# One decoder layer on one core: scores in larger groups, keys loaded ahead, probabilities in whole rows, padded products

## The chip, the cores and the metric

The kernel runs on one core of one Trainium2 chip. The metric is the device time of one execution in microseconds; the time before is the median of three runs.

## The reference

The kernel computes one layer of a hybrid decoder. There are two groups of tokens: a prompt of 512 tokens, and 8 running sequences with one new token each (the sample). All of it is float32. Cut to what matters:

```
def mixer_layer(x, s0, k_past, v_past, w_in, w_alpha2, b_alpha, gla_norm_g, w_out, ln_g, ln_b, rel_bias):
    h = jnp.einsum('btd,de->bte', x, w_in)
    qa, ka, va, za, ga, qb, kb, vb, gb = jnp.split(h, split_points, axis=-1)
    log_a = jax.nn.log_sigmoid((jnp.einsum('btr,rk->btk', za, w_alpha2) + b_alpha).astype(F32)) / GATE_TEMP
    o_a, s_new = gla_chunked(qa, ka, va, log_a, s0, chunk)
    o_a = o_a * lax.rsqrt(jnp.mean(jnp.square(o_a), axis=-1, keepdims=True) + RMS_EPS) * gla_norm_g.astype(F32)
    ...
        o_b = prompt_dilated(qb, kb, vb, rel_bias)
    ...
        o_b = dilated_attention(qb, k_all, v_all, q_idx, rel_bias)
    mix = jnp.concatenate([o_a * jax.nn.silu(ga.astype(F32)), o_b * jax.nn.silu(gb.astype(F32))], axis=-1)
    y = jnp.einsum('bte,ed->btd', mix.astype(x.dtype), w_out)
    x_new = layer_norm(DEEPNORM_ALPHA * x + y, ln_g, ln_b)
```

`gla_chunked` is gated linear attention with 4 heads; `dilated_attention` has 8 heads, each of which sees three patterns of past keys with a bias by distance. For the sample the keys and values of 1024 past tokens come from a cache; 256 of them fall into a pattern.

## The kernel before

**Planner.** The program's order is made on the host by `Plan`. Each piece of work is a generator (`Task`) with a priority; it yields operations, requests for a buffer (`Need`, or `Pair` for several at once) or waits for a mark (`At`). `Plan.run` goes through the tasks in order of priority, lets each take its buffers (`advance`), and issues the operation that by its own costs (`Op`) can start first. Every engine then executes its instructions in this fixed order. Line 359 in `Plan.issue` is where every instruction is issued, so nearly all rows of the profile have L359, and one goes by the names of the tiles. Nearly all DMAs are issued on SP, one queue, in order.

**Buffers.** `SLOTS` and `BANKS` are the supply: two raw weight buffers (`r`), six for their split halves (`w`), four 4 KB buffers for the sample (`sv`), three strips (`st`), four probability tiles (`pr`), and the eight PSUM banks as `d` 3, `s` 3, `t` 2.

**Products.** A float32 operand is split into a rounded high part (ACT, `hi`) and a low remainder (DVE, `lo`), and a product is three matmuls: high by high, high by low, low by high (`three`). `dense` is the backbone on PE: projections in the order ka, za, qa, qb, kb, vb, gb, va, ga over 8 tiles of the model dimension, then the output projection (`ps_yf`, `ps_y`). `first_loads` and `first_splits` bring x and the ka weights at the start. Everything else is put between the projections: GLA by levels (`ps_l`), state and output (`gla_state`, `gla_out`, `ps_oa`), and the attention of the prompt.

**Attention of the prompt.** `strips` loads a skewed bias strip per head; `scores` makes the scores (`ps_s`) of one feature tile, that is two heads, for query tiles 0 and 1 (`pi` 0) or 2 and 3 (`pi` 1), `softmax` follows with the bias, exponentials and transposes (`ps_pt`), `weighted` with the values (`ps_pv`).

**Attention of the sample.** `sample_queries` transposes the queries, writes them to DRAM (`qsd`), and per sequence loads them back to all partitions (`qbc`) with the past keys (`past`, 512 KB). GpSimd multiplies, DVE adds up (`lt`). `sample_softmax` makes the probabilities and writes them to DRAM (`psd_s`). `sample_values` loads per sequence the past values (`vv`) and the probabilities to all partitions (`pb`), GpSimd multiplies, DVE adds up (`o_pv`). The result enters the mix before the output projection. The loads of `pb` before, two per sequence for 64 partitions each:

```
            row = psd_s[bi * 8:bi * 8 + 8, :]
            for h2 in range(2):
                yield D.dma_start(pb[h2 * 64:h2 * 64 + 64],
                                  bass.AP(tensor=row.tensor, offset=row.offset + h2 * 256, ap=[[0, 64], [512, 4], [1, 256]]))
```

An access pattern is a list of pairs, step and count, the outermost first.

Of the kernel before, what the change touches and what calls it, by code (L numbers as in the profile page):

```python
# [48 lines left out]
C_W = 419  # L49
# [5 lines left out]

N_WARM = 8
# [133 lines left out]
class Plan:  # L190
# [173 lines left out]
def trunk(ctx: ExitStack, tc: tile.TileContext, xT, xp, xs, state, ck, cv, w_in, wab, gnorm,  # L364
# [23 lines left out]
    def rsqrt(o, x, scale, eps, between=None):  # L388
# [3 lines left out]
        yield V.tensor_scalar(x, x, scale, eps, op0=ALU.mult, op1=ALU.add)  # L392
        yield S.activation(o, x, AF.Ln)
        yield S.activation(o, o, AF.Exp, scale=-0.5)
        if between:

            add(between, 5)
            yield S.activation(t, o, AF.Square)
            yield S.mul(t, t, x)
            yield S.activation(t, t, AF.Copy, scale=-0.5, bias=1.5)  # L400
            yield S.mul(o, o, t)
        else:
            yield V.tensor_tensor(t, o, o, op=ALU.mult)
# [22 lines left out]
    rb = cst("rb", [66, NB, HB], F32R)  # L426
# [5 lines left out]
    q_s, k_s = cst("q_s", [P, 4, NB]), cst("k_s", [P, 4, NB])  # L432
    q_rows = cst("q_rows", [32, P])
    vnt, vat = cst("vnt", [P, 4, NB]), cst("vat", [P, 4, NB])
    lt = cst("lt", [P, 2, 64])
# [6 lines left out]
    psd_s = dram.tile([64, 256], F32, name="psd_s")  # L442
# [63 lines left out]
    def weight_loads():  # L506
        for g in order:
            for i in range(g.parts):
                yield from g.load(i)
# [26 lines left out]
    def first_loads():  # L536
        za = w_in[:, OFF["za"]:OFF["za"] + 16].rearrange("(k p) n -> p k n", p=P)
        for n, a, *b in FIRST:
# [10 lines left out]
            mark("first")  # L549
        yield D.dma_start(zw[:, :, :16], za)  # L550
# [3 lines left out]
        B["rb_raw"] = yield Need("t1", "rb_raw", [64, NB, HB])  # L554
        for i in range(2):
            yield D.dma_start(B["rb_raw"][i * 32:i * 32 + 32], rel_bias[:, None, :].to_broadcast([32, NB, HB]))
# [6 lines left out]
    def first_splits():  # L563
        for j, (n, a, *b) in enumerate(FIRST):
            yield At("first", j + 1)
            if n == "x":
# [6 lines left out]
                yield from split(xraw[a // 2][:, a % 2, c], xh[a][:, c], xl[a][:, c])  # L573
                mark("xs")
# [106 lines left out]
    def dense():  # L681
# [101 lines left out]
    def bias_table():  # L783
# [9 lines left out]
        yield At("rb")  # L793
        pt = yield bank("t", "ps_tab")
# [103 lines left out]
    def gla_state():  # L898
# [23 lines left out]
        plan.share(st, 3)  # L922
# [19 lines left out]
    def gla_queries():  # L942
# [12 lines left out]
        for h2 in range(2):  # L955
            plan.share(B[f"att{h2}"], 2)
        for u in range(2):
            yield from make(f"oa{u}", Need("g", f"oa{u}", [P, 2, 512]), 2)
            add(gla_out(u), 26 + u)

    def gla_out(u):

        yield At("st", 2 * u + 1)
        yield At("dg")
        va, att, qd = B[f"va{u}"], [B[f"att{h2}"] for h2 in range(2)], B["qa"]
        ps = yield Pair(*(bank("s", f"ps_oa{u}{h2}") for h2 in range(2)))
        po = {(h2, j, m): ps[h2][:, (2 * j + m) * P:(2 * j + m) * P + P] for h2 in range(2) for j in range(2) for m in range(2)}
        mm = Batch(T.matmul(po[h2, j, m], att[h2][:, (2 * u + j) * 2 + m, :], va[:, j, (m * 2 + h2) * P:(m * 2 + h2) * P + P],
                            start=j + m == 0, stop=False, skip_group_check=True) for h2 in range(2) for j in range(2) for m in range(2))
        mm += [T.matmul(po[h2, j, m], qd[h2 * 64:h2 * 64 + 64, m, (2 * u + j) * P:(2 * u + j) * P + P],  # L970
                        B["st"][h2 * 64:h2 * 64 + 64, 2 * u + j - 1, m, :], start=False, stop=j + m == 2, skip_group_check=True)
               for j in range(2) for m in range(2) for h2 in range(2) if u + j]
        yield mm
        free(qd, B["st"], *att)
        plan.share(va, 2)
        for h2 in range(2):
            plan.share(ps[h2], 2)
        for j in range(2):
            add(gla_head(u, j, ps, po), 26 + u + j / 2)
# [116 lines left out]
    def strips():  # L1096
        yield At("tab")
        yield At("qb", 1)
        for pi in range(2):
            w = 256 * (pi + 1)  # L1100
            for h in range(HB):
                yield At(f"kb{h // 2}{pi}")
                strip = yield Need("st", f"strip{h}{pi}", [P, w])
                plan.share(strip, 2)
# [6 lines left out]
    def scores(m, pi, qt):  # L1111
# [9 lines left out]
        for v in range(2):  # L1121
            yield At(f"strip{2 * m + v}{pi}")
        yield At(f"qb{m}{pi}")
        for u in range(pi + 1):
            yield At(f"kb{m}{u}")
        every = [(v, q) for v in range(2) for q in (qt if own else qt[:1])]
        pr = yield Pair(*(Need("pr", f"pr{2 * m + v}{q}", [P, (q + 1) * P if own else n]) for v, q in every))
        ps = yield Pair(*(bank(("s", "d"), f"ps_s{2 * m + v}{q}") for v, q in every))
        pr, ps = ({(v, q): z[every.index((v, q if own else qt[0]))] for v in range(2) for q in qt} for z in (pr, ps))
        kp, qx = B[f"kp{m}"], [B[f"q{x}{pi}"] for x in "hl"]  # L1130
        yield Batch(T.matmul(ps[v, q][:, cols[q]], qx[a][v * 64:v * 64 + 64, m, (q % 2) * P:(q % 2) * P + P],
                             kp[v * 64:v * 64 + 64, b, :(q + 1) * P], start=i == 0, stop=i == 2, skip_group_check=True)
                    for q in qt for i, (a, b) in enumerate(((0, 0), (0, 1), (1, 0))) for v in range(2))
        free(kp, *qx)
        for v in range(2):
            if not own:
                plan.share(ps[v, qt[0]], len(qt))
                plan.share(pr[v, qt[0]], len(qt))
            for q in qt:
                add(softmax(2 * m + v, q, ps[v, q], pr[v, q], cols[q]), 31 + 20 * pi / 100 + m / 50)  # L1140
# [70 lines left out]
    def sample_queries():  # L1211
        yield At("qb", 8)
        yield from sample_rows(q_s, q_rows)
        yield D.dma_start(by_tile(qsd), q_rows)
        for bi in range(NB):
            qbc = yield Need("t2", f"qbc{bi}", [P, 512])
            yield D.dma_start(qbc, qsd[bi:bi + 1, :].to_broadcast([P, 512]))
            past = yield Need("sv", f"past{bi}", [P, 2, 512])
            yield D.dma_start(past, ck[bi])
            add(sample_logit(bi, past, qbc), 50)  # L1220

    def sample_logit(bi, past, qbc):
# [4 lines left out]
        yield V.tensor_reduce(lt[:, :, bi * 8:bi * 8 + 8], past.rearrange("p k (h d) -> p k h d", d=64), axis=AX.X, op=ALU.add)  # L1227
# [3 lines left out]
    def sample_softmax():  # L1231
        yield At("kb", 8)
        yield At("lt", 5)
        sel = yield Need("t1", "sel", [64, C_AV - C_E2])
        yield D.dma_start(sel, c_f[:64, C_E2:C_AV])
        e2, pnm, m32 = sel[:, :P], sel[:, C_PN - C_E2:C_PN - C_E2 + 32], sel[:32, C_LN - C_E2:]
# [7 lines left out]
        l32 = yield Need("t1", "l32", [32, NB * HB])  # L1244
        yield V.tensor_reduce(ln_new, prod.rearrange("p (h d) -> p h d", d=64), axis=AX.X, op=ALU.add)
        free(prod)
        yield V.tensor_tensor(l32.rearrange("p (r u) -> p r u", u=2), ln_new[:, None, :].to_broadcast([32, 32, 2]),
# [9 lines left out]
        yield T.matmul(ps[:64, :258], rb.rearrange("p b h -> p (b h)"), cts, start=True, stop=False, skip_group_check=True)  # L1257
        yield T.matmul(ps[:64, 256:257], l32, one[:32], start=False, stop=False, skip_group_check=True)
# [456 lines left out]
```

## Time and profile before

| | |
|---|---|
| median of three runs | 289.32 us (288.43 to 290.51) |
| profiled execution | 288.67 us |
| its span | 286.8 us |
| PE busy | 275.0 us, 96% |
| DVE, ACT, GpSimd busy | 225.7, 167.5, 55.9 us |
| granted TensorE clock | 0.994 |
| DMA | 51.18 MB, mean 178 GB/s |
| first matmul to last | 1.20 us to 279.26 us |

The profile is of one execution. The span goes from its first to its last instruction; the device time is longer by what lies around it. PE is TensorE, PEld its weight loads, DVE, ACT, POOL and SP the vector, scalar, GpSimd and sync engines. A window row gives for a stretch its length, the busy time of each engine with the count of instructions, the granted clock, the mean share of 16 DMA engines and what they moved. Float32 products without a split appear as two matmuls each.

### The profile page before, as it was taken

The page shows a single profiled execution, that of the slowest core. Times are in us where ns is not written, and L with a number is a line of the kernel's source. Part 1 is how long each engine was busy: PE and PEld are TensorE (multiplying, and loading weights), DVE is VectorE, ACT ScalarE, POOL GpSimd, SP SyncE. Part 2 cuts the span into 40 slices and gives each one's busy share as a digit, 9 for nine tenths or more (in the row PEclk, how much of TensorE's full clock was granted, in tenths as well). Part 3 has the DMA queues.
Part 4 walks back from the last instruction along what each step waited for, and adds up shares of the span by engine and source line. Part 5 has one row for each costly group of instructions (what it writes and reads, how often), then busy time and mean ns, then how long its engine had stood idle before and what let it go on. Part 6 is the DMA issues. An engine that isn't in the chain of part 4 may idle for free.

```text
span 286.8 us, 6896 instructions
## 1 busy us (share of the span) xinstructions
PE 275.0 (96%) x2636; PEld 259.5 (90%) x2636; DVE 225.7 (79%) x547; ACT 167.5 (58%) x478; POOL 55.9 (19%) x74
## 2 busy tenths in 40 slices
PE   8999999999999998999999999999999999999990
PEld 5899999998989998899989999999999999997880
DVE  3846897999889968988889997864888995339745
ACT  5757664554567777566869867526689774113201
POOL 4000001000782444401604444540000000000000
PEclk9999999999999999999999999999999999999997
DMA  7966522225866797648998987559754788741211
GB/s 209 269 191 195 147 75 75 75 78 167 296 201 222 196 287 230 175 130 243 274 201 188 239 227 219 149 149 228 221 95 148 230 297 252 111 151 73 78 75 73
DMA packets 58936, 51.18 MB, mean 178 GB/s; under 512 B 12555, under 2 KB 50197, under 8 KB 58903
## 3 DMA queue, kind: packets, MB, share of 16 engines
q1 hardware_dynamic: 58794, 50.66, 63.2%
q8 instruction: 21, 0.34, 0.5%
q14 instruction: 13, 0.10, 0.1%
q10 hardware_dynamic: 108, 0.07, 0.1%
HBM read 45.17 MB, written 6.03 MB: 179 GB/s over the span
## 4 chain that ended last, share of the span: by engine, by line
PE 71%; DVE 13%; DMA 8%; ACT 5%; issue 2%; SPq 1%; DVEq 0%; ACTq 0%
PE ps_qb L359 8%; PE ps_yf L359 8%; PE ps_y L359 8%; PE ps_ga L359 6%; PE ps_kb L359 4%; PE ps_qa L359 4%; PE ps_gb L359 4%; PE ps_va L359 4%; PE ps_ka L359 4%; DMA raw_gb__2152<-in_w_in_dram 3%; DMA out_dram<-feat 3%; PE ps_pt L359 2%; PE ps_va_f L359 2%; PE ps_l L359 2%; PE ps_s L359 2%; PE ps_pv L359 2%
## 5 line engine op out<-in xcount | busy, mean ns | idle before, releaser
L359 POOL TENSOR_TENSOR vv<-vv,pb 128x256 f32<-128x256 f32 x32 | 26.1, 846 | 45.5 <-DMA pb<-psd_s 39.8
L359 POOL TENSOR_TENSOR past<-past,qbc 128x256 f32<-128x256 f32 x32 | 25.6, 831 | 43.4 <-DMA past<-in_ck_dram 36.0
L359 ACT ACTIVATE pr<-pr,ms 128x128 f32<-128x128 f32 (+3 forms) x49 | 26.1, 546 | 5.8 <-DVE ms L359 5.2
L359 PE MATMUL ps_pt<-cf,pr 128*128 128x128 f32 x80 | 14.1, 280 | 1.4 <-DVE pt L359 1.0
L359 DVE CUSTOM_DVE_ANT_0 pr<-ps_s,strip 128x128 f32<-128x128 f32 (+3 forms) x32 | 14.3, 476 | 0.0
L359 PE MATMUL ps_ka<-xx,hi_ka 128*128 128x264 f32 (+1 forms) x64 | 13.5, 307 | 0.3 <-DVE xx L359 0.3
L359 ACT ACTIVATE sg<-sg 128x264 f32<-128x264 f32 (+1 forms) x32 | 13.4, 419 | 0.2
L359 PEld LDWEIGHTS ps_ka<-xx,hi_ka 128*128 128x128 f32 x64 | 11.0, 205 | 1.2 <-DVE xx L359 0.8
L359 DVE TENSOR_TENSOR ptl<-ps_pt,pth 128x384 fp32r<-128x384 f32 (+1 forms) x16 | 9.8, 617 | 2.8 <-ACT pth L359 2.8
L359 PEld LDWEIGHTS ps_pt<-cf,pr 128*128 128x128 f32 x80 | 9.0, 140 | 3.3 <-DVE pt L359 1.6
L359 ACT ACTIVATE d<-d 128x512 f32<-128x512 f32 x13 | 7.8, 637 | 6.7 <-DVE d L359 6.7
L359 ACT COPY feat_y<-ps_yf 128x256 f32<-128x256 f32 x8 | 3.0, 371 | 12.7 <-PE ps_yf L359 12.7
L359 ACT ACTIVATE rstd<-mv 128x1 f32<-128x1 f32 x4 | 0.7, 199 | 15.9 <-DVE mv L359 15.9
L359 POOL MEMSET att<- 64x512 f32 x2 | 1.0, 523 | 44.5 <-DVE ks L359 44.5
L359 ACT CAST pth<-ps_pt 128x384 fp32r<-128x384 f32 (+1 forms) x16 | 8.4, 534 | 2.2 <-PE ps_pt L359 2.0
L359 DVE TENSOR_REDUCE o_pv<-vv 128x4 f32<-128x1024 f32 x8 | 9.7, 1212 | 0.0
L359 DVE TENSOR_REDUCE lt<-past 128x16 f32<-128x1024 f32 x8 | 9.6, 1199 | 0.0
L359 PE MATMUL ps_ka<-xx,lo_ka 128*128 128x264 f32 (+1 forms) x32 | 9.4, 295 | 0.0
L359 DVE TENSOR_TENSOR obT<-ps_pv,pvl 64x256 f32<-64x256 f32 x16 | 6.6, 415 | 3.5 <-ACT pvl L359 3.3
L359 DVE TENSOR_TENSOR xx<-x_raw,xx 128x520 fp32r<-128x520 f32 (+2 forms) x9 | 5.8, 640 | 4.6 <-ACT xx L359 4.6
L359 ACT COPY pvl<-ps_pv 64x256 f32<-64x256 f32 x16 | 5.5, 370 | 6.1 <-PE ps_pv L359 5.3
L359 DVE TENSOR_TENSOR d<-b 128x1024 f32<-128x1024 f32 x7 | 8.5, 1218 | 0.0
(535 smaller groups left out, 1092.4 us busy)
## 6 DMA issues: line engine op xcount, KB each, us to landing
past<-in_ck_dram SPq DMA_DIRECT2D x8, 512.0 KB
vv<-in_cv_dram SPq DMA_DIRECT2D x8, 512.0 KB
pb<-psd_s SPq DMA_DIRECT2D x16, 256.0 KB
qbc<-qsd SPq DMA_DIRECT2D x8, 256.0 KB
strip<-tabr SPq DMA_DIRECT2D x8, 256.0 KB
y<-in_xp_dram SPq DMA_DIRECT2D x4, 512.0 KB
x_raw<-in_xT_dram SPq DMA_DIRECT2D x7, 260.0 KB
out_dram<-y SPq DMA_DIRECT2D x3, 512.0 KB
```

The lines of the kernel that those rows point to most:

```text
L359: getattr(eng.eng, op.fn)(*op.args, **op.kw)
```

## The change

- `Plan.run`: when a task's step frees a buffer, the pass through the tasks starts again from the first in line.
- `first_splits`, `dense`: x tiles 1 and 2 are split in two halves as tile 0 was (`N_HALF`), and the ka products that need the low part of x come last in each step. The first weight group after ka is loaded ahead of `zw`.
- `scores`, `strips`: for `pi` 0 two feature tiles, four heads, in one batch, with four banks and four `pr` at once; two heads' strips share a buffer.
- `gla_out`: both halves in one batch with four banks.
- `sample_queries`: the first four `past` are loaded once the first qb tile is there, ahead of the queries' way through DRAM.
- `sample_softmax`, `sample_values`: `psd_s` is laid out by sequence and half, written in two DMAs, and each `pb` is one load for 128 partitions in rows of 4 KB.
- The small products `ps_sl`, `ps_pn`, `ps_ms`, `ps_vs` are padded to 128 by 128, with tiles cleared or widened for it (`rb`, `lt`, `sel`, `l32`, `pn_r`, `sums`, `avg`).
- `rsqrt` for the last normalisation has one ACT instruction less; the bias table's product waits for the first qa result; `a_s` takes the place of `la_s`.

```
-            for t in sorted(self.tasks, key=lambda t: (t.prio, t.seq)):
-                if not self.advance(t):
+            line = sorted(self.tasks, key=lambda t: (t.prio, t.seq))
+            self.freed = True
+            while self.freed:
+
+                self.freed = False
+                for t in line:
+                    self.advance(t)
+                    if self.freed:
+                        break
...
+            yield V.tensor_scalar(x, x, eps, -0.5, op0=ALU.add, op1=ALU.mult)
+            yield S.activation(o, x, AF.Ln, scale=-2.0)
+            yield S.activation(o, o, AF.Exp, scale=-0.5)
             add(between, 5)
             yield S.activation(t, o, AF.Square)
-            yield S.mul(t, t, x)
-            yield S.activation(t, t, AF.Copy, scale=-0.5, bias=1.5)
+            yield S.activation(t, t, AF.Copy, scale=x, bias=1.5)
             yield S.mul(o, o, t)
...
+        yield from order[0].load(0)
         yield D.dma_start(zw[:, :, :16], za)
...
-                yield from split(xraw[a // 2][:, a % 2, c], xh[a][:, c], xl[a][:, c])
-                mark("xs")
+                for c in (c,) if b or a >= N_HALF else TS:
+                    yield from split(xraw[a // 2][:, a % 2, c], xh[a][:, c], xl[a][:, c])
+                    mark("xs")
...
-                yield At("xs", k + 1 + (u if k == 0 else 1))
-                for i in range(2):
-                    yield from three(pk[i, u][:, :TW[u]], k, halves(k, u, groups[f"ka{i}"]))
+                yield At("xs", 2 * k + 1 + u if k < N_HALF else k + 1 + N_HALF)
+
+                for last in (False, True):
+                    for i in range(2):
+                        pairs = halves(k, u, groups[f"ka{i}"])
+                        for j in (1,) if last else (0, 2):
+                            yield T.matmul(pk[i, u][:, :TW[u]], *pairs[j], start=k == 0 and j == 0, stop=k == KT - 1 and last)
...
     def sample_queries():
-        yield At("qb", 8)
-        yield from sample_rows(q_s, q_rows)
-        yield D.dma_start(by_tile(qsd), q_rows)
+        yield At("qb", 2)
+        pasts = []
         for bi in range(NB):
-            qbc = yield Need("t2", f"qbc{bi}", [P, 512])
-            yield D.dma_start(qbc, qsd[bi:bi + 1, :].to_broadcast([P, 512]))
+            if bi == 4:
+                yield At("qb", 8)
+                yield from sample_rows(q_s, q_rows)
+                yield D.dma_start(by_tile(qsd), q_rows)
+                for i, past in enumerate(pasts):
+                    yield from sample_query(i, past)
             past = yield Need("sv", f"past{bi}", [P, 2, 512])
             yield D.dma_start(past, ck[bi])
-            add(sample_logit(bi, past, qbc), 50)
+            if bi < 4:
+                pasts.append(past)
+            else:
+                yield from sample_query(bi, past)
...
-        yield T.matmul(ps[:64, :258], rb.rearrange("p b h -> p (b h)"), cts, start=True, stop=False, skip_group_check=True)
-        yield T.matmul(ps[:64, 256:257], l32, one[:32], start=False, stop=False, skip_group_check=True)
+        yield T.matmul(ps[:, :258], rb.rearrange("p b h -> p (b h)"), cts, start=True, stop=False, skip_group_check=True)
+        yield T.matmul(ps[:, 256:257], l32, one, start=False, stop=False, skip_group_check=True)
...
-        yield D.dma_start(psd_s, p_s[:, :256])
+
+        for h2 in range(2):
+            src = bass.AP(tensor=p_s.tensor, offset=p_s.offset + h2 * p_s.ap[0][0], ap=[[2 * p_s.ap[0][0], 32], [1, 256]])
+            yield D.dma_start(psd_s[:, h2].rearrange("b (m k) -> b m k", m=4), src)
...
-            row = psd_s[bi * 8:bi * 8 + 8, :]
-            for h2 in range(2):
-                yield D.dma_start(pb[h2 * 64:h2 * 64 + 64],
-                                  bass.AP(tensor=row.tensor, offset=row.offset + h2 * 256, ap=[[0, 64], [512, 4], [1, 256]]))
+            row = psd_s[bi]
+            yield D.dma_start(pb, bass.AP(tensor=row.tensor, offset=row.offset, ap=[[1024, 2], [0, 64], [1, 1024]]))
...
-            if h % 2 == 0:
-                for qt in ((2, 3) if pi else (0, 1),):
-                    add(scores(h // 2, pi, qt), 31 + 20 * pi / 100 + h / 100)
+            if h % (2 if pi else 4) == 0:
+                add(scores((h // 2,) if pi else (h // 2, h // 2 + 1), pi, (2, 3) if pi else (0, 1)), 31 + 20 * pi / 100 + h / 100)
```

More of the change, by code (lines that the diff above doesn't have):

```diff
@@ L441, in trunk @@
     qsd = dram.tile([NB, 512], F32, name="qsd")
[L442 removed]
+    psd_s = dram.tile([NB, 2, 1024], F32, name="psd_s")
     B = {}
@@ L506, in weight_loads @@
     def weight_loads():
-        for g in order:
+        for g in order[1:]:
             for i in range(g.parts):
@@ L1120, in scores @@
         own = pi
[L1121 to L1135, printed above, removed]
+        heads = [2 * m + v for m in ms for v in range(2)]
@@ new lines, in scores @@
+        for h in heads:
+            yield At(f"strip{h}{pi}")
+        for m in ms:
+            yield At(f"qb{m}{pi}")
+            for u in range(pi + 1):
+                yield At(f"kb{m}{u}")
+        every = [(h, q) for h in heads for q in (qt if own else qt[:1])]
+        pr = yield Pair(*(Need("pr", f"pr{h}{q}", [P, (q + 1) * P if own else n]) for h, q in every))
+        ps = yield Pair(*(bank(("s", "d"), f"ps_s{h}{q}") for h, q in every))
+        pr, ps = ({(h, q): z[every.index((h, q if own else qt[0]))] for h in heads for q in qt} for z in (pr, ps))
```

136 lines of the change are left out of this document (82 added, 54 removed).

## The prediction

> **What bounds the kernel now.** I read the page first, then the waits of PE, then windows of stages, and last the chain that ended last.
>
> ```profile
> span 286.8 us, 6896 instructions
> PE 275.0 (96%) x2636; PEld 259.5 (90%) x2636; DVE 225.7 (79%) x547; ACT 167.5 (58%) x478; POOL 55.9 (19%) x74
> PE 71%; DVE 13%; DMA 8%; ACT 5%; issue 2%; SPq 1%; DVEq 0%; ACTq 0%
> ```
>
> PE is busy 96% of the span, and 71% of the chain is PE. An edit gains only if it takes time out of PE's stream or closes one of its few gaps; it loses as soon as PE's next operand comes late. The profiled execution took 288.67 us, 1.87 us more than its span and 0.65 us under the median of the three runs, 289.32 us; the sum below is made against 288.67.
>
> The gaps are small. Where operands came late, it was behind a DMA:
>
> ```profile
> 2.60 3.77 DMA x_raw<-in_xT_dram
> ...
> 102.77 8.52 DMA out_dram<-feat
> 111.28 0.02 issue
> 111.31 0.37 ACT pvl L359
> 111.68 0.52 ACT hi_vb__1819 L359
> ...
> 113.58 0.88 DVE lo_vb__1820 L359
> ...
> 132.90 9.72 DMA raw_gb__2152<-in_w_in_dram
> ```
>
> Columns: start, duration, what. A transfer with little ahead of it takes 3.77 us; the weight load at 132.90 took 9.72 us, because it was issued behind four probability loads:
>
> ```profile
> 129.56 1.32 SPq L359 DMA_DIRECT2D pb<-psd_s  x2
> 130.97 0.55 SPq L359 DMA_DIRECT2D vv<-in_cv_dram  x1
> 131.62 1.23 SPq L359 DMA_DIRECT2D pb<-psd_s  x2
> 132.90 0.60 SPq L359 DMA_DIRECT2D raw_gb__2152<-in_w_in_dram  x1
> ```
>
> So nearly all loads go through SP's one queue, and a weight load waits for what stands ahead of it. This decides the forecast. The windows that I need (length, busy times, clock, DMA share, GB/s):
>
> ```profile
> 27.00:28.00 1.00, 1.00 (x10) 1.00 (x9) 0.97 (x4) 0.76 (x2) 0.00 (x0) 1.00 0.52 205
> 252.40:254.00 1.60, 1.60 (x15) 1.60 (x15) 0.17 (x1) 0.37 (x1) 0.00 (x0) 1.00 1.01 399
> 126.40:182.00 55.60, 55.12 (x459) 52.50 (x458) 49.94 (x118) 40.70 (x105) 19.14 (x25) 1.00 0.88 220
> 100.00:110.00 10.00, 10.00 (x89) 9.99 (x88) 7.51 (x22) 7.29 (x24) 2.94 (x4) 1.00 0.98 282
> 110.00:120.00 10.00, 8.65 (x67) 7.39 (x66) 9.21 (x20) 5.46 (x16) 6.92 (x8) 1.00 0.70 212
> 40.00:60.00 20.00, 20.00 (x386) 19.59 (x386) 17.64 (x27) 9.70 (x19) 1.05 (x2) 1.00 0.29 78
> 110.00:240.00 130.00, 127.87 (x1104) 122.23 (x1103) 110.42 (x285) 91.24 (x267) 33.00 (x40) 1.00 0.75 202
> ```
>
> **The parts that should gain.** First, the start. The halved splits of x tiles 1 and 2, with the product that needs the low part put last:
>
> ```profile
> 6.39 0.62 ACT L359 CAST xx<-x_raw 128x520 fp32r<-128x520 f32 x1 [0.76 <-DMA x_raw<-in_xT_dram]
> 7.05 0.70 DVE L359 TENSOR_TENSOR xx<-x_raw,xx 128x520 fp32r<-128x520 f32 x1 [0.96 <-ACT xx L359]
> 7.07 0.39 PE L359 MATMUL ps_ka<-xx,hi_ka 128*128 128x264 f32 x1
> 7.80 0.39 PE L359 MATMUL ps_ka<-xx,hi_ka 128*128 128x264 f32 x1 [0.34 <-DVE xx L359]
> ```
>
> PE issues one product of tile 1 at 7.07 and stands until DVE has the low part, 7.80. With halves, ACT has the first at about 6.8, four products need only high parts of x (4 x 0.12 = 0.48 us), and DVE's first half is there by 7.3: 0.7 us. Tile 2 gives 0.2 more. I take 0.9 (0 to 1.2). The price, two more instructions each on ACT and DVE, lies under PE's first 10 us. The weight load put ahead of `zw` delays that by 512 KB, 1.3 us at 399 GB/s; its products start 9.7 us after its issue:
>
> ```profile
> 8.56 0.38 SPq L359 DMA_DIRECT2D zw<-in_w_in_dram  x1
> ...
> 18.30 1.98 PE ps_za L359 x62
> ```
>
> Second, visits to another matmul shape (rows by columns of the array):
>
> ```profile
> 82.80 5.28 PE ps_kb L359 x44
> 88.08 0.89 PE ps_s L359 x12
> ...
> 123.64 0.90 PE ps_sl L359 x7
> ...
> 200.98 2.43 PE ps_oa L359 x24
> ```
>
> A full product of about 256 columns costs 5.28/44 = 0.12 us. The twelve score products run as six pairs, three of 256 and three of 128 columns, 0.54 us of work in 0.89: a visit costs up to 0.35 us, entry and exit together. The change saves seven: two by joining feature tiles in `scores`, one by joining the halves in `gla_out`, four by padding (`ps_sl`, `ps_pn`, `ps_ms`, `ps_vs`). At 0.2 to 0.35 each that is 1.4 to 2.5; I take 1.6, since `ps_sl` has only 0.90 us in all.
>
> Third, the keys ahead: four loads of 512 KB move into 40 to 60 us, where DMA is busy 0.29, out of the traffic that fills it to 0.98 in 100 to 110. Its victim is the store that landed after 8.52 us, held ACT's `pvl` and cost PE 1.35 us in 110 to 120. I take 1.0 (0 to 1.35).
>
> Fourth, the end:
>
> ```profile
> 281.41 0.29 ACT L359 ACTIVATE newton<-newton,mv 128x1 f32<-128x1 f32 x1
> 281.74 0.20 ACT L359 ACTIVATE newton<-newton 128x1 f32<-128x1 f32 x1
> 281.97 0.29 ACT L359 ACTIVATE rstd<-rstd,newton 128x1 f32<-128x1 f32 x1
> ```
>
> One of these three goes, the plain one, 281.97 - 281.74 = 0.23 us on the path to the last store.
>
> At nothing I put the three memsets, the wider `rb`, `sel` and `avg`, `a_s` in place and the table's later product: small work of DVE, SP or PE far from its consumer. Four banks and four `pr` at once delay `softmax`, which PE bridges with projections; its last transposes lie 52 us ahead of the output projection that needs them:
>
> ```profile
> 178.03 0.46 PE ps_pt L359 x4
> ...
> 230.00 2.69 PE ps_yf L359 x22
> ```
>
>  Giving freed buffers to the first in line reorders anything by a little: I put it at 0 (+-2 us): it can't win more than PE's idle time, 130.00 - 127.87 = 2.1 us in the longest window above, and I allow as much for a loss. Gains together: 0.9 + 1.6 + 1.0 + 0.2 = 3.7 us.
>
> **The part that loses.** `sample_values` replaces 16 loads of `pb`, each with 64 rows in its outermost loop, by eight whose source is `[[1024, 2], [0, 64], [1, 1024]]`: an outermost loop of **two**. How many DMA engines does such a load get? The nearest row is `tabr`, whose source has an outermost loop of 8 (heads):
>
> ```profile
> 23.91 0.77 SPq L359 DMA_DIRECT2D tabr<-tab  x1
> 27.08 0.38 SPq L359 DMA_DIRECT2D raw_qb__434<-in_w_in_dram  x1
> ...
> 250.11 0.93 SPq L359 DMA_DIRECT2D y<-in_xp_dram  x2
> ```
>
> Between 27.00 and 28.00 `tabr` is alone in flight, and the DMA share stands at 0.52 with 205 GB/s: 8 of 16 engines, each at 205/(0.52 x 16) = 24.6 GB/s. The `y` loads, 128 rows outermost, fill all: 1.01 at 399 GB/s, 24.7 each. So a loop of eight got eight engines, full speed each; read in the same way a loop of two gets two. I take two; the other end is 16.
>
> [...]
>
> Then each `pb`, 524,288 bytes, is 262,144 on each of two engines: 10.6 us at 24.6 GB/s, and eight take **85 us** on these two. They also carry a sixteenth of the rest. In 126.40 to 182.00, 220 GB/s x 55.6 us = 12.2 MB moved, 4.2 MB of it `pb`; the rest, 8.0 MB, is 0.50 MB per engine: 20 us at 24.6 GB/s, 32 at this stage's own 220/(0.88 x 16) = 15.6; I take 26. So the two engines need 85 + 26 = 111 us for a stage of 55.6: +55. Two things move this. PE has up to two weight groups in hand, 48 products of 0.12 = 5.8 us each, so 0 to 12 less; and the plan, to which whole rows are cheap (`Op` rates them 340 instead of 175), packs the eight closer, so their stage has less PE work to hide under: up to 12 more. I take -6 and +6. Behind a late `pb` stand POOL's products, DVE's `o_pv` reductions in order with everything else of DVE, and the weight loads on SP's queue, so PE stops with them. POOL already waits there:
>
> ```profile
> POOL vv L359 <- DMA pb<-psd_s: 39.8, 6, 16.7
> ```
>
> **Sum:** 288.67 - 3.7 + 55 = 340; against the median 340.6, so 341 us.
>
> **Rivals.**
> 1. *All sixteen engines carry the new load.* For it: every load with 128 or 64 rows outermost; against it: the 0.52. Then whole rows relieve the stage, and the gains stand: 288.67 - 3.7 + 0.65 less perhaps 0.4 for the wait behind `raw_gb`, 285 us, **faster**. Chance 0.11. It decides if the share of the `pb` stage stays above half.
> 2. *Eight engines, as `tabr`.* 65,536 bytes each, 2.7 us a load, 21 us for eight instead of 10.6: some 5 us lost of the gains, 290 us. Nothing gives eight from a loop of two. Chance 0.03.
> 3. *Two engines, but well hidden.* If the loads start near 110 and the plan and the buffers let every other load flow around them, only the total counts: 110 to 240 moves 26.3 MB, 22.1 without `pb`, 1.38 MB per engine, 56 us; 56 + 85 = 141 for 130: +11, 296 us. Against it: four `sv` buffers allow two `pb` in flight, and each weight load queues behind one. Chance 0.14.
> 4. *Worse than the sum.* 20 GB/s instead of 24.6 (105 us for eight), 32 us of other traffic, and eight packed into 38 us: +99, 384 us. Chance 0.15.
>
> **How the numbers follow.** My case has 0.57 and its own range is 322 to 362 (288.67 - 3.7 + 85 + 20 - 55.6 - 12 below; the gains at nothing, 85 + 32 - 55.6 + 12 above). Cases 3 and 4 are slower too: 0.57 + 0.14 + 0.15 = 0.86 slower. Within 1%, about what a measurement of this kernel tells from no change, is case 2: 0.03. Faster is case 1: 0.11. The range reaches from under most of case 3 to case 4: 300 to 385.
>
> **What would show it.** Right: in the page of the changed kernel POOL's wait for `pb` grows from 39.8 to well over 60 us; the DMA share of that stage falls to 0.2 to 0.5 while weight loads land 10 us and more after issue; PE, 96% busy before, falls near 80%, its gaps of several microseconds each ending on split weights or on DVE work behind `o_pv`; before the first `pb`, `ps_ka` ends about 0.9 us earlier. Wrong: a share near 1 under `pb` loads that land in about 4 us, with the span near 283.

## The result, and the profile after

The changed kernel takes **352.66 us** (median of six runs, 350.99 to 355.62) where the kernel before takes 289.44: ratio 1.220, interval 1.2134 to 1.226. It is slower by 63 us; I had said 341.0. The profiled execution shown here took 355.62 us, with a span of 353.8.

From the page of the changed kernel: its first part, the granted clock by slices, the shares of the chain, and the load in question:

```profile
span 353.8 us, 6882 instructions
...
PE 286.6 (81%) x2636; PEld 271.8 (77%) x2636; DVE 221.6 (63%) x548; ACT 168.6 (48%) x480; POOL 53.1 (15%) x74
...
PEclk9999999999999999995695586985889999999997
...
PE 39%; DMA 30%; DVE 17%; ACT 5%; POOL 3%; issue 3%; SPq 3%; POOLq 0%; DVEq 0%
...
pb<-psd_s SPq DMA_DIRECT2D x8, 512.0 KB
```

PE fell from 96% to 81% of the span, and the chain that was 71% PE is now 39% PE and 30% DMA. The number of matmuls is the same, 2636. The waits of the changed kernel name the place:

```profile
POOL vv L371 <- DMA pb<-psd_s: 113.7, 8, 31.7
...
DVE o_pv L371 <- POOL vv L371: 67.9, 8, 13.0
...
PE ps_pt L371 <- ACT pr L371: 16.1, 1, 16.1
```

GpSimd waited 39.8 us for `pb` before, 113.7 now, for all eight loads. Behind it stands DVE (67.9 us at `o_pv`), and behind DVE, in its order, what PE needs. The longest of PE's waits shows the way, each row with the idle time before it and what ended that:

```profile
164.65 2.76 POOL L371 TENSOR_TENSOR vv<-vv,pb 128x256 f32<-128x256 f32 x4 [12.58 <-DMA pb<-psd_s]
...
167.44 1.22 DVE L371 TENSOR_REDUCE o_pv<-vv 128x4 f32<-128x1024 f32 x1 [13.01 <-POOL vv L371]
168.58 0.15 DVE L371 RECIPROCAL ms<-ms 128x1 f32<-128x1 f32 x1
...
168.82 0.61 ACT L371 ACTIVATE pr<-pr,ms 128x384 f32<-128x384 f32 x1 [16.51 <-DVE ms L371]
...
169.49 0.47 PE L371 MATMUL ps_pt<-cf,pr 128*128 128x128 f32 x1 [16.06 <-ACT pr L371]
```

`ms` belongs to the attention of the prompt and does not need `pb`; it only stands behind `o_pv` in DVE's order. ACT waits for it, and PE for ACT.

The chain between 139 and 194 (start, duration, what) shows two of the eight turns:

```profile
139.69 24.79 DMA pb<-psd_s
...
164.65 2.77 POOL vv L371 x4
...
168.69 25.09 DMA pb<-psd_s
```

Each of these two loads takes 25 us, GpSimd's four products 2.8 us, and the load between them was issued at 160.71, before the first had landed. Two windows of the same trace (length, busy times, clock, DMA share, GB/s):

```profile
133.80:250.50 116.70, 69.04 (x475) 65.93 (x474) 46.63 (x114) 39.34 (x100) 19.44 (x28) 0.77 0.37 113
160.00:170.00 10.00, 0.51 (x3) 0.51 (x4) 2.56 (x6) 1.18 (x3) 2.76 (x4) 0.50 0.42 139
```

The first runs from the issue of the first `pb` to the landing of the last. PE is busy 69.04 of 116.70 us, while the mean share of the 16 DMA engines is 0.37: on average ten of them have nothing to do. The products with `pb`, before and after, in the rows by tile (first and last start in us):

```profile
L359 POOL TENSOR_TENSOR vv<-vv,pb x32: 724/744/1587, 134.8 to 189.0; 128x256 f32<-128x256 f32 x32
```

```profile
L371 POOL TENSOR_TENSOR vv<-vv,pb x32: 715/722/737, 149.3 to 252.7; 128x256 f32<-128x256 f32 x32
```

54 us became 103. The semaphore events in the trace (when a load's semaphore was counted up) tell more than the share. A weight load gets 16 increments. Of the one issued at 217.57, fourteen came between 5.29 and 6.22 us after the issue, the other two at 17.80 and 19.96; of the one issued at 187.24, fourteen by 10.49 us, two at 21.71 and 22.93. I read this as fourteen engines free and two full. A `pb` gets three increments: one early, after 0.9 to 1.7 us, two at the end (0.94, 20.95 and 22.16 us for the fifth). The landings of the eight `pb` lie 14.5 us apart on average, from 149.1 to 250.5. In the trace of the kernel before, `tabr`, with its outermost loop of eight, has nine: one after 1.18 us, eight between 5.09 and 5.61.

Two increments at the end fit two engines, as eight fit the 0.52 of `tabr`; that each of them stands for an engine is my reading. The share fits that too: from 224 to 226, with the `pb` issued at 213.10 in flight and the weight load of 217.57 short of its last two increments, it is 0.12 at 47 GB/s, that is 0.12 x 16 = 1.9 engines.

### The profile page after: what moved, and what is told of

The parts are those of the page before. It is cut to its first block, busy times and chain, and to the rows that moved or that the text cites. A ratio compares the mean times of both kernels' runs of the same rounds, so it can differ in the third digit from the quotient of the medians.

```text
span 353.8 us, 6882 instructions
## 1 busy us (share of the span) xinstructions
PE 286.6 (81%) x2636; PEld 271.8 (77%) x2636; DVE 221.6 (63%) x548; ACT 168.6 (48%) x480; POOL 53.1 (15%) x74
## 4 chain that ended last, share of the span: by engine, by line
PE 39%; DMA 30%; DVE 17%; ACT 5%; POOL 3%; issue 3%; SPq 3%; POOLq 0%; DVEq 0%
DMA pb<-psd_s 26%; PE ps_yf L371 7%; PE ps_y L371 6%; PE ps_qb L371 5%; PE ps_qa L371 3%; PE ps_vb_f L371 3%; POOL vv L371 3%; SPq L371 3%; DMA x_raw<-in_xT_dram 2%; PE ps_ka L371 2%; PE ps_vb L371 2%; PE ps_va L371 2%; DVE pr L371 1%; DVE near L371 1%; DVE d L371 1%
## 5 line engine op out<-in xcount | busy, mean ns | idle before, releaser
L371 DVE TENSOR_REDUCE o_pv<-vv 128x4 f32<-128x1024 f32 x8 | 9.8, 1221 | 67.9 <-POOL vv L371 67.9
L371 POOL TENSOR_TENSOR past<-past,qbc 128x256 f32<-128x256 f32 x32 | 26.7, 866 | 86.1 <-DMA qbc<-qsd 76.0
L371 POOL TENSOR_TENSOR vv<-vv,pb 128x256 f32<-128x256 f32 x32 | 22.2, 724 | 113.7 <-DMA pb<-psd_s 113.7
L371 PE MATMUL ps_pt<-cf,pr 128*128 128x128 f32 x80 | 15.2, 299 | 16.9 <-ACT pr L371 16.1
L371 PEld LDWEIGHTS ps_pt<-cf,pr 128*128 128x128 f32 x80 | 10.4, 153 | 17.5 <-ACT pr L371 16.3
L371 PE MATMUL ps_pv<-ptl,vhl 128*64 128x256 f32 (+1 forms) x32 | 8.2, 300 | 15.7 <-DVE ptl L371 15.7
L371 PEld LDWEIGHTS ps_pv<-ptl,vhl 128*64 128x64 f32 x32 | 4.9, 154 | 16.2 <-DVE ptl L371 16.2
L371 ACT ACTIVATE sg<-sg 128x264 f32<-128x264 f32 (+1 forms) x32 | 13.3, 416 | 0.2
L371 PE MATMUL ps_s<-kp,qh 64*128 64x128 f32 (+3 forms) x64 | 9.0, 353 | 4.4 <-DVE gb L371 4.4
L371 PE MATMUL ps_va_f<-xx,lo_va__2961 128*128 128x264 f32 x8 | 3.0, 374 | 9.7 <-DVE lo_va__2961 L371 9.7
L371 PEld LDWEIGHTS ps_s<-kp,qh 64*128 64x128 f32 x64 | 5.4, 191 | 5.7 <-DVE gb L371 4.8
L371 PEld LDWEIGHTS ps_va_f<-xx,lo_va__2961 128*128 128x128 f32 x8 | 2.1, 263 | 9.9 <-DVE lo_va__2961 L371 9.9
```

Source lines behind the costliest of these rows:

```text
L371: getattr(eng.eng, op.fn)(*op.args, **op.kw)
```

## The experiments

Four questions, in the order in which they came up: is it the loop of two; what happened to the gains that I had summed; does one part of the change carry that loss; by which way does it reach PE. "The base" is the changed kernel with each `pb` in two loads.

**Is it the outermost loop of two?**

*e1*: the changed kernel, each `pb` in two loads, rows still whole (4 KB), outermost loop 64.

```
-            yield D.dma_start(pb, bass.AP(..., ap=[[1024, 2], [0, 64], [1, 1024]]))
+            for h2 in range(2):
+                yield D.dma_start(pb[h2 * 64:h2 * 64 + 64], bass.AP(..., offset=row.offset + h2 * 1024, ap=[[0, 64], [1, 1024]]))
```

> The changed kernel with each pb loaded in two halves of 64 partitions, outermost loop 64 instead of 2, same whole rows of 4 KB, same layout in DRAM. Theory (the outermost loop of two puts a load on two engines, and this is the whole loss): pb lands within 5 us, the DMA share of the pb stage is above 0.7, the time is 284 to 290 us. Rival (another part of the change, such as the new order of tasks or the group of four heads, costs time in the same stage): the time stays above 300 us.

Measured: 295.63 us, ratio 1.021 (1.0153 to 1.0274). 57.0 of the 63.2 us are gone, with the same bytes in rows of the same length. But 6.2 us remain, where the theory had a gain. A load now lands after 3.4 to 12.6 us, not always within 5 as expected; the DMA share from 126.4 to 182 is 0.85.

*e2*: the kernel before, with only the layout of `psd_s` and the load of `pb` as in the change.

```
-        yield D.dma_start(psd_s, p_s[:, :256])
+        for h2 in range(2):
+            src = bass.AP(..., offset=p_s.offset + h2 * p_s.ap[0][0], ap=[[2 * p_s.ap[0][0], 32], [1, 256]])
+            yield D.dma_start(psd_s[:, h2].rearrange("b (m k) -> b m k", m=4), src)
...
-            row = psd_s[bi * 8:bi * 8 + 8, :]
-            for h2 in range(2):
-                yield D.dma_start(pb[h2 * 64:h2 * 64 + 64], ...)
+            row = psd_s[bi]
+            yield D.dma_start(pb, bass.AP(..., ap=[[1024, 2], [0, 64], [1, 1024]]))
```

> The kernel before with only the probabilities as in the change: psd_s by sequence and half, written in two DMAs, pb in one load with an outermost loop of two. Theory: this alone makes the loss, 342 to 356 us, POOL waiting above 100 us for pb. Rival (the loss needs the new order or the keys ahead as well): below 330 us.

Measured: 349.31 us, ratio 1.207 (1.2022 to 1.2126). The load alone makes a loss of 60 us, as the theory said.

*e3*: the changed kernel, each row of `psd_s` written twice, so that the loop is four.

```
-            ap=[[1024, 2], [0, 64], [1, 1024]]
+            ap=[[1024, 4], [0, 32], [1, 1024]]
```

> The changed kernel with each probability row written twice, so that pb is one load with an outermost loop of four (rows of 4 KB, 32 partitions each). Theory (as many engines as the loop has steps): 131,072 bytes on each of four engines, 5.3 us at 24.6 GB/s plus about 4 us of other traffic, eight in some 74 us instead of the 117 us of the changed kernel: 298 to 312 us. Rival 1 (it is the reading of one row by many partitions that is slow, not the count of engines): 340 us and more. Rival 2 (four are as good as sixteen, since the stage has slack): at most 290 us.

Measured: 309.12 us, ratio 1.070 (1.0644 to 1.0754), inside the theory's range. The eight loads take 79.2 us from first issue to last landing (74 expected). The waits of GpSimd in e2, e3 and e1:

```profile
POOL vv L359 <- DMA pb<-psd_s: 107.1, 8, 25.3
```

```profile
POOL vv L371 <- DMA pb<-psd_s: 60.4, 6, 28.8
```

```profile
POOL vv L371 <- DMA pb<-psd_s: 28.9, 6, 8.7
```

In the changed kernel a loop of 2, 4 and 64 gives 113.7, 60.4 and 28.9 us of waiting (107.1 for 2 in the kernel before), and 3, 5 and 16 semaphore increments for a load. Bytes and rows are the same; the outermost loop decides. In e1 there are also twice as many loads, and the planner rates them differently; with the rating of the changed kernel (e6 below) the time is 294.35 us, so the rating is not what brings the 57 us back.

*e4*: the changed kernel with the old `psd_s` and the old loads, rows of 1 KB.

```
-            yield D.dma_start(pb, bass.AP(..., ap=[[1024, 2], [0, 64], [1, 1024]]))
+            for h2 in range(2):
+                yield D.dma_start(pb[h2 * 64:h2 * 64 + 64],
+                                  bass.AP(..., offset=row.offset + h2 * 256, ap=[[0, 64], [512, 4], [1, 256]]))
```

> The changed kernel with the old layout and loads of the probabilities (16 loads, rows of 1 KB, outermost loop 64). Theory: rows of 1 KB and of 4 KB move the same bytes on 16 engines, so within 2 us of the version with two loads of 64 partitions. Rival (whole rows do help when all engines carry them): 2 to 5 us above it.

Measured: 297.28 us, ratio 1.027 (1.0223 to 1.0319). Against e1 (1.0153 to 1.0274) whole rows bring at most little: the difference of 1.65 us lies within the intervals. And the rest of the change, without any edit at `pb`, loses 8 us, so the remaining 6 us of e1 do not come from its loads either.

**Where did the gains go?** In e1 PE is ahead at the end of the projections (the last `ps_ga` ends at 227.91, before 230.00) and behind at the end of the first output products (263.30 against 255.79). Windows of the kernel before, then of e1:

```profile
220.00:230.00 10.00, 9.70 (x104) 9.13 (x104) 8.74 (x36) 8.49 (x32) 0.00 (x0) 1.00 0.64 185
230.00:245.00 15.00, 15.00 (x126) 15.00 (x126) 11.38 (x22) 8.45 (x21) 0.00 (x0) 1.00 0.84 259
```

```profile
220.00:230.00 10.00, 10.00 (x86) 10.00 (x86) 8.52 (x31) 7.93 (x28) 0.00 (x0) 1.00 1.07 332
230.00:245.00 15.00, 10.54 (x90) 8.83 (x90) 12.43 (x31) 9.65 (x27) 0.00 (x0) 0.86 0.61 172
```

The loss of e1 is here: 4.46 us of idle PE from 230 to 245, and a lower clock after it. Of the next four kernels three take one part out of e1 each, and e6 changes only a rating of the planner.

*e5*: `gla_out` in two batches again.

```
-        add(gla_out(), 26)
+            add(gla_out(u), 26 + u)
...
-        yield At("st", 3)
+        yield At("st", 2 * u + 1)
```

> The base of these four is the changed kernel with each pb in two loads of 64 partitions (295.63 us). Here gla_out is put back to one batch for each half, with two banks each. In the base PE is 2.1 us ahead of the kernel before at the last ps_ga (227.91 against 230.00) and 7.5 us behind at the last ps_yf (263.30 against 255.79): the loss lies between 200 and 245, where sixteen squares of gla_head stand in ACT's queue ahead of the splits of ga, SP waits 13.7 us for lo_ga with the second v loads behind it, and ps_og, the sample's output, comes at 236 instead of 221. Theory (the joined batch brings those sixteen squares at once): 286 to 290 us, SP's wait for lo_ga under 9 us, ps_og before 228. Rival (the planner's rating of the pb loads gave another order there, and the joined batch has nothing to do with it): 294 to 297 us.

Measured: 294.38 us, 1.0175 (1.0114 to 1.0236). SP's wait for the same split is 12.1 us, and `ps_og` comes at 233.7, not before 228. My theory fell: neither sign came, and the difference to e1, 1.25 us, lies within the intervals.

*e6*: the planner's rating of the two loads, nothing else.

```
-            rate = 60 if run <= 128 else 175 if x.ap[0][1] <= 64 else 340 if run >= 4096 else 230
+            rate = 60 if run <= 128 else 340 if run >= 4096 else 175 if x.ap[0][1] <= 64 else 230
```

> Base with one edit: the planner rates the two pb loads of 4 KB rows at 340 as it rates the one load of the changed kernel, not at 175 with 0.6 us more; so the order of the work is near that of the changed kernel, and the loads use all engines. In the changed kernel, which was already 65 us late, ps_og came 0.5 us after the first of the last ps_ga products had its operands and ps_yf followed ps_ga at once (297.19, 297.03). Theory of the joined batch: no change, 293 to 298. Rival (the rating's order makes the 6 us): 286 to 290 us, ps_og before 228.

Measured: 294.35 us, 1.0181 (1.011 to 1.0252). The time is that of no change, but not for that theory's reason: `ps_og` came early, at 228.2, nearly as the rival had it, and the time did not follow. The idle time went elsewhere:

```profile
160.00:180.00 20.00, 14.97 (x99) 13.80 (x99) 13.56 (x32) 11.03 (x28) 11.44 (x15) 0.83 0.92 226
220.00:240.00 20.00, 18.80 (x174) 17.89 (x173) 18.11 (x59) 18.33 (x62) 0.00 (x0) 1.00 0.62 185
```

The same operations on the same data, in an order that differs because one constant of the planner differs, moved a hole of about 5 us from near 240 to near 170.

*e7*: no restart of the pass when a buffer is freed.

```
-            line = sorted(self.tasks, key=lambda t: (t.prio, t.seq))
-            self.freed = True
-            while self.freed:
...
-            for t in line:
-                if not t.heads:
+            for t in sorted(self.tasks, key=lambda t: (t.prio, t.seq)):
+                if not self.advance(t):
```

> Base with the planner's loop as before: a freed buffer does not restart the pass through the tasks. The base starts the levels of gated linear attention 5.4 us later than the kernel before (first ps_l 50.20 against 44.82), and from 60 to 100 PE is idle 2.45 us where it was 0.64. Theory (the restart costs only what lies in those windows, about 1.8 us, and the loss after 200 is the joined batch): 293 to 296 us. Rival (the restart is the cause of the whole 6 us): 286 to 290 us.

Measured: 297.81 us, 1.0273 (1.0205 to 1.0341). That is above both ranges, and against e1 the intervals overlap: no cost of the restart is seen. The first `ps_l` is still at 50.06, so the late levels are not its doing.

*e8*: scores and strips by one feature tile again.

```
...
-            if h % (2 if pi else 4) == 0:
-                add(scores((h // 2,) if pi else (h // 2, h // 2 + 1), pi, ...
+            if h % 2 == 0:
+                add(scores((h // 2,), pi, ...
```

> Base with scores and strips of query tiles 0 and 1 by one feature tile (two heads) as before. My prediction had the joining worth two visits to another matmul shape, 0.4 to 0.7 us. Theory: 295 to 297.5 us, and PE's idle time from 60 to 100 stays near 2.4 us. Rival (four banks and four pr at once hold up PE in 60 to 100): 292 to 294.5 us, and the idle time falls to about 1 us.

Measured: 294.07 us, 1.0167 (1.01 to 1.0234). This is the rival's time, and PE's idle time from 60 to 100 fell to 1.02 us as it had said; but against e1 the intervals overlap. That joining saves visits is not seen in the time.

**Does one part of the change carry the 6 us?** Three kernels add one part alone to the kernel before, with its lines of the change as they stand above; none of them touches `pb`. The restart of the pass alone was not run on the kernel before.

*e9*: start and tail (`N_HALF`, order of the ka products, first qa weights ahead of `zw`, table later, shorter `rsqrt`).

```
+        yield from order[0].load(0)
         yield D.dma_start(zw[:, :, :16], za)
...
+                for c in (c,) if b or a >= N_HALF else TS:
...
-            yield S.mul(t, t, x)
-            yield S.activation(t, t, AF.Copy, scale=-0.5, bias=1.5)
+            yield S.activation(t, t, AF.Copy, scale=x, bias=1.5)
```

> The kernel before (289.4 us) with two parts of the change alone: the start (half splits of x tiles 1 and 2, low product last, first qa weights ahead of zw, table after the first qa result) and the shorter rsqrt of the last normalisation. My prediction gave them 0.9 and 0.23. Theory of the prediction: 288.0 to 288.8 us, last ps_ka before 17.6 (18.30 before). Rival (this start also moves the order behind it: in the runs so far with it the first ps_l comes 5 us later, 50 against 44.8, and the sample's chain ends late): 291 to 296 us, first ps_l near 50, last o_pv after 195 (189.7 before).

Measured: 301.79 us, 1.0428 (1.038 to 1.0476), above even the rival's range. The rival's two signs came: the first `ps_l` is at 50.18 (46.27 in e10, 45.01 in e11, 44.82 before), and the last `o_pv` at 220.5. So the late levels come with the new start.

*e10*: scores by two tiles, `gla_out` in one batch, padded products.

```
-    def scores(m, pi, qt):
+    def scores(ms, pi, qt):
...
-            add(gla_out(u), 26 + u)
+        add(gla_out(), 26)
...
-        yield T.matmul(ps[:64, :258], rb.rearrange("p b h -> p (b h)"), cts, ...
+        yield T.matmul(ps[:, :258], rb.rearrange("p b h -> p (b h)"), cts, ...
```

> The kernel before with only the parts that save visits to another matmul shape: scores of query tiles 0 and 1 by two feature tiles, both halves of gla_out in one batch, padded products. My prediction gave them 1.6 us. Theory of the prediction: 287.0 to 288.6 us. Rival (the joined batches hold banks and bring work to ACT and DVE at once, the two undone one by one gave 1.2 and 1.6 us back within the interval): 290 to 294 us, PE idle time in 60 to 100 near 2 us instead of 0.64.

Measured: 302.72 us, 1.0452 (1.0412 to 1.0493), far above both ranges, though PE's idle time from 60 to 100 is only 0.86 us.

*e11*: only `sample_queries`, the first four `past` ahead.

```
-        yield At("qb", 8)
+        yield At("qb", 2)
...
+            if bi == 4:
+                yield At("qb", 8)
+                yield from sample_rows(q_s, q_rows)
+                yield D.dma_start(by_tile(qsd), q_rows)
```

> The kernel before with only the first four past loads ahead of the queries' way through DRAM. My prediction gave this 1.0 us (0 to 1.35). Theory of the prediction: 288.0 to 289.0 us, and the store of feat near 102 lands in under 5 us (8.52 before). Rival (nothing waits for these keys: in all runs GpSimd's first product waits for qbc, 80 us in total): 289 to 290 us, PE idle in 100 to 120 still over 1 us (1.35 before).

Measured: 295.78 us, 1.0218 (1.0173 to 1.0263), above both ranges.

Each part alone loses more than all of them together without the loop of two (6.2 us), or as much. So the 6 us are no sum of prices. In their own places three parts do about what I had said. In e9 the last `ps_ka` ends at 17.64 instead of 18.30, and with the shorter `rsqrt` the time from the last matmul to the span's end is 7.26 us, before 7.54. In e10 the visits are cheaper, counted from the first product of a visit to the first product behind it: 24 score products in one visit take 1.58 us, two visits of 12 took 0.89 each; `ps_oa` 5.20 in one, before 2.52 and 2.97; `ps_pn` 0.14 for 0.23, `ps_ms` and `ps_vs` 0.14 for 0.20 each. With the two joinings of score products that is 0.9 us without `ps_sl`. For the keys ahead no gain is shown: in e11 PE is busy 19.85 of the 20 us from 100 to 120, before 18.65, but in e10, without them, 20.00, and e11's store of `feat` still landed only after 7.38 us. What was gained is lost later. Three rows by tile, each for the kernel before, e11, e1, e10 and e9: the last sum over the sample's values, the loads of the sample's state (the second one is the last number before the semicolon), and its product.

```profile
L359 DVE TENSOR_REDUCE o_pv<-vv x8: 1200/1212/1222, 141.0 to 189.7; 128x4 f32<-128x1024 f32 x8
...
L359 SPq DMA_DIRECT2D s<-in_state_dram x2: 377/475/573, 192.6 to 204.2; - x2
...
L359 PE MATMUL ps_og<-s,qx x32: 272/273/297, 220.7 to 221.6; 128*32 128x128 f32 x32
```

```profile
L359 DVE TENSOR_REDUCE o_pv<-vv x8: 1207/1210/1222, 143.4 to 203.2; 128x4 f32<-128x1024 f32 x8
...
L359 SPq DMA_DIRECT2D s<-in_state_dram x2: 371/482/593, 197.0 to 214.0; - x2
...
L359 PE MATMUL ps_og<-s,qx x32: 272/273/298, 228.6 to 229.6; 128*32 128x128 f32 x32
```

```profile
L371 DVE TENSOR_REDUCE o_pv<-vv x8: 1206/1213/1222, 148.8 to 205.9; 128x4 f32<-128x1024 f32 x8
...
L371 SPq DMA_DIRECT2D s<-in_state_dram x2: 385/476/568, 191.2 to 218.5; - x2
...
L371 PE MATMUL ps_og<-s,qx x32: 272/273/297, 236.2 to 237.0; 128*32 128x128 f32 x32
```

```profile
L359 DVE TENSOR_REDUCE o_pv<-vv x8: 1204/1212/1222, 157.7 to 216.6; 128x4 f32<-128x1024 f32 x8
...
L359 SPq DMA_DIRECT2D s<-in_state_dram x2: 425/496/567, 194.8 to 227.1; - x2
...
L359 PE MATMUL ps_og<-s,qx x32: 272/273/297, 241.7 to 243.5; 128*32 128x128 f32 x32
```

```profile
L360 DVE TENSOR_REDUCE o_pv<-vv x8: 1204/1212/1221, 158.2 to 220.5; 128x4 f32<-128x1024 f32 x8
...
L360 SPq DMA_DIRECT2D s<-in_state_dram x2: 368/451/534, 195.0 to 226.2; - x2
...
L360 PE MATMUL ps_og<-s,qx x32: 272/273/297, 242.5 to 243.3; 128*32 128x128 f32 x32
```

The last `o_pv` at 189.7, 203.2, 205.9, 216.6 and 220.5 goes with 289.5, 295.8, 295.6, 302.7 and 301.8 us. By and large, the later the sample's work ends, the longer the kernel. It is a tendency and no law: e6 (195.8 and 294.35 us) has its hole before 180 instead, e8 (210.5 and 294.07 us) is faster than its place in the row, and e11 has its longest hole (2.24 us) already at 147, at a `ps_pt`.

**By which way does a late sample hold PE?**

*e12*: e1, in which the output projection does not wait for the sample's gated linear attention; its columns are zeros, and `ps_og` comes after the last `ps_yf`.

```
+        yield At("yts", KT)
         og = yield bank(("s", "t"), "ps_og")
...
-        mark("o_as")
...
-        yield At("o_as")
+        yield V.memset(o_as, 0.0)
```

> Base is the changed kernel with each pb in two loads of 64 partitions (295.63 us), whose ps_og comes at 236.16 and whose output projection starts at 227.75 and stands until 243.5. Here the output projection does not wait for the sample's gated linear attention: its columns enter the mix as zeros, and ps_og and what follows it come after the last ps_yf; all else of that chain still runs. Left out: the sample's gated linear attention in the output. Theory (the late end of the sample's chain is what costs): the last ps_yf before 258 (263.30 in the base, 255.79 in the kernel before), 287 to 291 us. Rival (the weights of the output projection are just as late, behind the same queues of SP, ACT and DVE): 293 to 297 us, PE idle over 4 us from 230 to 250.

Measured: 294.37 us, 1.0157 (1.0104 to 1.0209). The rival was right. From 230 to 245 PE is busy 10.69 us, 10.54 in e1, and from 230 to 250 it is idle 4.31 us. The timelines of PE and of SP's queue in e12:

```profile
236.08 0.28 PE L371 MATMUL ps_yf<-mlb,hi_wo__3658 128*128 128x264 f32 x1
239.34 0.39 PE L371 MATMUL ps_yf<-mhb,hi_wo__3690 128*128 128x264 f32 x1 [2.98 <-ACT hi_wo__3690 L371]
```

```profile
218.19 0.57 SPq L371 DMA_DIRECT2D s<-in_state_dram  x1
218.81 2.89 SPq L371 DMA_DIRECT2D v<-vad  x2
221.81 1.18 SPq L371 DMA_DIRECT2D raw_wo__3447<-in_w_out_dram  x1
...
233.70 0.39 SPq L371 DMA_DIRECT2D raw_wo__3660<-in_w_out_dram  x1
```

PE waits for weights: the split of `raw_wo` issued at 233.70. In the kernel before, the state and `v` are loaded at 204 to 206, ahead of all output weights but the first. Here they come at 218 to 222 between them, the weight load at 221.81 takes 7.9 us to land, and the DMA share from 220 to 230 is 1.09 (0.64 before). The split of the load at 221.81 ends only at 233.67, between state updates of the sample (`s`) on ACT and DVE; then its buffer is free, and the load at 233.70 can go out. It lands at 237.51, but ACT starts its split at 238.67, because it waits 2.00 us for DVE at an operation ahead of it. So I read that the sample's late loads and updates push the output weights back, on SP's queue, in the DMA engines and in the order of ACT and DVE; a kernel with these loads at their old place was not run. That the result itself is late matters less in e1: without that wait the last `ps_yf` comes 2.9 us earlier (260.38), and 1.3 us show in the time, within the intervals.

Not settled: which single choice of the planner moves the sample's work in each kernel. The orders differ too much for one cause to be named, and no kernel here fixes the order by hand. No run beat the kernel before.

## Why the prediction was right or wrong

**The loss, right.** The two engines (the share of 0.12 from 224 to 226), and the way behind them, came as I worked out. I had 111 us for the two engines in the `pb` stage, 13.9 a load; they took 116.7 from first issue to last landing, with landings 14.5 apart. From the share of that stage the two terms can be estimated apart: 0.37 x 16 x 116.7 = 691 us of engine time; if two engines were busy throughout, the other fourteen had (691 - 233)/14 = 33 us each of other traffic, and 116.7 - 33 = 84 us are left for `pb`. I had 85 for `pb`, and 26 for the rest, which was too little. I had +55 us; undoing the loop alone gives 57.0 (e1), making it alone 59.7 (349.31 less 289.63, the kernel before measured with it). Rival 2, eight engines, falls with the share of 0.12 and the 349 us of e2; rival 3, two engines well hidden, with the time, and with e3, where even a loop of four took 309 us. The two corrections of 6 us that I set against each other, weights in hand and a denser plan, were not measured; that 55 and 57.0 lie so close is in part luck. Rival 4 had eight loads packed into 38 us; `vv` waits for buffers, and the eight issues stretched over 97 us (133.83 to 231.04).

**The signs, right but one.** GpSimd's wait 113.7 us (over 60 foretold), DMA share 0.37 (0.2 to 0.5), PE 81% (near 80), seven weight loads issued between 134 and 243 landing after 10.8 to 22.9 us (10 and more), six holes of PE from 4.4 to 16.1 us, 52.7 us together. The one that failed is the start: the last `ps_ka` ends at 18.43, not 0.9 us earlier. In this execution a tile of x landed 1 us later than before; but over the ten traces with the new start it ends at 17.2 to 18.4, over the four without at 18.3 to 19.0, about 0.6 us apart on average.

**The gains, wrong, and why.** The step that failed is "I put it at 0 (+-2 us)" for the reordering, and with it "Gains together: 0.9 + 1.6 + 1.0 + 0.2 = 3.7 us". Without the loop of two the change takes 6.2 us more, not 3.7 less: 9.9 us off. That and the 2.0 us of the loss term (57.0 for 55) are nearly all of the 12.0 us between the sum, 340.6, and 352.7. I had priced each edit where it stands and bounded the reordering by PE's idle time before, 2.1 us. That bound is for a gain; for a loss I wrote "I allow as much", with no reason. And I had asked it of one edit only, the freed buffers, for which e7 shows no cost. The 1.0 us for the keys had a wrong reading in it too: the store of `feat` that they were to relieve landed after 7.38 us instead of 8.52. But every edit changes the times that the planner computes, and so the order of all that follows. e9, e10 and e11 cost 12.3, 13.3 and 6.3 us, while of the local gains 0.66, 0.27 and 0.9 us could be read. That the new order makes these costs is argued: e6 shows that order alone can move a hole of 5 us, but no kernel here holds the order fixed.

**Rival 1** had 285 us if all sixteen engines carried the load. e1 is that case for the engines, as I read its 16 increments a load and its DMA share of 0.85, and it took 295.63: the gains that failed are in that sum too.

## What to carry to other kernels

Read the outermost loop of a broadcast load's source before its row length: here 2, 4 and 64 rows outermost gave 353, 309 and 296 us with the same bytes, and weight loads issued among those with a loop of two landed after 10.8 to 22.9 us. Where a planner lays out the whole program by estimated times, price an edit as a new order and not only in its place: parts forecast to gain about 1 us each cost 6 to 13 us. Look for a chain with little slack (here, it seems, the sample's, whose loads came between those of the output weights when it was late) and check that an edit leaves its end where it was.

## What was not expected of the hardware

In the changed kernel and in e1 the granted clock fell to 0.50 when PE had waited, and stayed there into the work that followed. In e1, around the holes between 237 and 243.5:

```profile
237.37:240.78 3.41, 0.95 (x4) 0.60 (x4) 2.84 (x6) 2.25 (x7) 0.00 (x0) 1.00 0.76 257
240.78:244.19 3.41, 1.97 (x7) 1.33 (x7) 2.52 (x10) 1.60 (x5) 0.00 (x0) 0.50 0.81 146
...
243.50:247.50 4.00, 3.95 (x18) 3.95 (x19) 0.69 (x3) 1.46 (x3) 0.00 (x0) 0.50 0.86 301
247.50:250.00 2.50, 2.50 (x23) 2.50 (x22) 1.03 (x3) 0.37 (x1) 0.00 (x0) 0.98 0.96 172
```

PE is busy nearly throughout the last two, with 18 matmuls in 4.0 us at a granted clock of 0.50, and 23 in 2.5 us at 0.98: 0.22 against 0.11 us each. The holes thus cost more than their length, by an estimate from these two rows 18 x 0.11 = 2 us more. In the changed kernel PE's busy time grew from 275.0 to 286.6 us for the same number of matmuls, 2636: 11.6 of the 67.0 us by which the span is longer. In e1, without the long waits, it is 276.1. I had not counted that. Up to its last matmul the changed kernel has five stretches at half clock, from 157.64, 184.94, 212.25, 236.15 and 253.21, of 17.07, 20.48, 6.83, 10.24 and 6.83 us: 5, 6, 2, 3 and 2 times 3.41. In the 3.41 us ahead of each of them PE was busy for 0.00 us. From 229.32 to 232.73 it was idle for 1.84 us, and the clock stayed at 1.00 in the 3.41 us behind. In e1 it was idle for 2.46 us from 237.37 to 240.78, in no hole longer than 2.26 us, and the clock behind was 0.50.
